# Where the weight tiles of a two-layer decoder trunk start in SBUF: offsets per weight unit, two spare tiles and one small tile removed

## The chip, the cores and the metric

The kernel runs on one core of one Trainium2 chip. The metric is the device time of one execution in microseconds (us); three runs of the kernel before gave 2567.21, 2567.60 and 2567.82 us, so the median is 2567.6 us. Five engines work side by side: TensorE (PE) multiplies matrices, ScalarE (ACT), VectorE (DVE) and GpSimd (POOL) do the elementwise work, and SyncE (SP) issues most transfers. In the profile PE has two rows: PE for the matmuls that stream a moving operand, and PEld for the loads of the stationary operand (LDWEIGHTS). Operands of both lie in SBUF, which has 128 partitions; an address below is the byte at which a tile starts in each of them. A difference of 0.2% (5.1 us) is about what a measurement of this kernel can tell from no change.

## The reference, cut to what matters

Each of two layers is a half-step feed-forward block, a mixer (attention and a state-space branch, merged by gates) and a second half-step feed-forward block. All of it is in float32; the sequence has 512 tokens, the model width is 1024, the hidden width of a feed-forward block 2816.

```python
def swiglu(h, w_up, w_down):
    gate, up = jnp.split(h @ w_up, 2, axis=-1)
    return (jax.nn.silu(gate) * up) @ w_down
...
for l in range(DEPTH):
    x = x + 0.5 * swiglu(rms_norm(x, ffn1_norm[l]), ffn1_w_up[l], ffn1_w_down[l])
    h = rms_norm(x, mix_norm[l])
    proj = h @ w_in[l]
    ...
    merged = jax.nn.sigmoid(gate_sb) * y_sb + jax.nn.sigmoid(gate_ssm) * y_ssm
    x = x + merged @ w_out[l]
    x = x + 0.5 * swiglu(rms_norm(x, ffn2_norm[l]), ffn2_w_up[l], ffn2_w_down[l])
return rms_norm(x, final_norm)
```

## The kernel before, in words

**Two halves of every operand.** Each float32 operand is held as a pair: a rounded part (`hi`, type float32r) and the rest (`lo`). A product is three matmuls into one PSUM tile (`mm3`, lines 348 to 352): L350 is `hi` times `hi`, L351 has the weights' `lo`, L352 the activations' `lo`.

**Weight units.** All weights are cut into units of at most 128 x 1024 elements, used in the order of `unit_order`. `fetch` (from L267) issues each unit's DMA into a `wraw` tile. `convert` (from L301) then writes the unit's two parts: ACT copies it to `hi` (L315, tile `whi`), DVE subtracts to get `lo` (L317, tile `wlo`). `whi` and `wlo` are tiles of the pool `wsp`, three of each, 4096 bytes per partition. `unit` hands the pair to the caller; `ahead` keeps two units converted in advance. In most stages a 128-column slice of the unit is the stationary operand and 512 columns of an activation move past it. The exceptions are the projections of v and z (`by_tokens`), where the unit moves and the activation is stationary.

**The pairs of feed-forward blocks.** 40 pairs of hidden blocks are computed with a fast matrix multiplication of seven products (`pair_of_blocks`, L604 to L677). Each product is a unit of its own, called a part: "11", "12", "s2", "s1", "s3", "s4", "22". A part has 24 matmuls of 256 moving columns (2 hidden blocks x 4 slices x 3). In parts 11, 12 and s4 the moving operand is a half of a normalised activation tile (`hhi`, `hlo`); in s2, s1, s3 and 22 it is a sum or difference of such halves (`th`, `tl`). The first part goes to PSUM tile `mm`, 12 to another `mm`, s2 and s3 to the first again, s1 and s4 to a `pa` tile, 22 to the first `mm`. For some parts the weights are themselves sums, made in tiles `s1`, `s2`, `s3` (group `s` in the profile) by POOL's accumulating DMA (L284) or DVE (L298).

**Where tiles start.** Pools are stacked from the left end of SBUF, or, where `side="right"` is given, from the right end downwards. From the left come constants, `nrm`, then `hp` (eight `hhi`, eight `hlo`), `wraw`, `wsp`, and after it whatever the stage needs: in a feed-forward block `act` and small tiles, in the mixer the gates and the pool `mp`. From the right come the eight `x` tiles, then a spare tile `rim` of 320 bytes that nothing reads or writes (L1431), then `th`, `tl`, `uv` and the sums `s`. In the mixer the right side holds instead a spare tile `edge` of 384 bytes (L1334), the attention outputs `ohi`, `olo` and 24 tiles `yt`. The built program gives these starts:

| tile | first start in bytes | remainder by 256 |
|---|---|---|
| `hhi` / `hlo` | 26208 / 42592 | 96 |
| `wraw` | 58976 | 96 |
| `whi` / `wlo` | 71264 / 83552 | 96 |
| `act` (feed-forward), first gate tile (mixer) | 95840 | 96 |
| merged `mhi` / `mlo` | 104032 / 120416 | 96 |
| sums `s` | 151200 | 160 |
| `th`, `tl` (lowest) | 171680 | 160 |
| `yt` (lowest) | 163424 | 96 |
| `ohi` / `olo` | 212576 / 220768 | 96 |
| `x` (lowest) | 212960 | 224 |

All tiles of one name lie whole multiples of 256 bytes apart, and so do the slices that a matmul takes of them (128 columns are 512 bytes), so one remainder holds for all matmuls with that tile.

**Attention.** `attention` (from L938) keeps softplus sums for four key blocks. The shortest block, 128 columns, has its two parts in one tile `short` of `mp`; matmuls L1005 and L1007 read it. Tiles `state` of `mp` (two of 768 bytes) are used later, by the state-space groups.

Of the kernel before, what the change touches and what calls it, by code (L numbers as in the profile page):

```python
# [9 lines left out]
F32R = mybir.dt.float32r  # L10
# [7 lines left out]
P = 128  # L18
SEQ = 512
NT = SEQ // P  # L20
DM = 1024
KB = DM // P
# [7 lines left out]
GW = HPG * HD  # L30
# [143 lines left out]
class Builder:  # L174
# [114 lines left out]
    def add(self, key):  # L289
# [8 lines left out]
        self.nc.vector.tensor_tensor(r, a, b, op=ALU.add)  # L298
        yield 1

    def convert(self, i):  # L301

        nc = self.nc
        key = self.keys[i]
        n = self.units[key][1] * P
        raw, self.raw[i] = self.raw[i], None
        if key[-1] in ("s1", "s3"):
            raw = self.sums[key] if key[-1] == "s1" else self.sums.pop(key)
        elif key[-1] in ("s2", "s4"):
            while key[2:] == ("pair", 0, "s4") and key not in self.sums:  # L310
                yield 1
            raw = self.sums[key[:-1] + ("s2",)]
        hi = self.t(self.wsp, [P, KB * P], "whi", F32R)
        lo = self.t(self.wsp, [P, KB * P], "wlo", F32R)
        nc.scalar.copy(hi[:, :n], raw[:, :n])  # L315
        yield 2
        nc.vector.tensor_tensor(lo[:, :n], raw[:, :n], hi[:, :n].bitcast(F32), op=ALU.subtract)  # L317
        self.loaded[i] = (hi, lo)
        if key[2:] == ("pair", 0, "s2"):
            self.spawn(self.onto(key[:-1] + ("s4",), raw), 2)  # L320
# [148 lines left out]
    def opening(self, gain):  # L469

        nc, n = self.nc, 2 * P
        raws, w = self.raw, []
        self.raw, self.loaded = [None, None], [None, None]
        for _ in raws:
            w.append((self.t(self.wsp, [P, KB * P], "whi", F32R), self.t(self.wsp, [P, KB * P], "wlo", F32R)))
        ps = [self.t(self.pa, [P, SEQ], "pa") for _ in raws]
        for k in range(KB):
            for i, (raw, (hi, lo)) in enumerate(zip(raws, w)):
                if k % 2 == 0:
                    cs = slice(k * P, k * P + n)  # L480
                    nc.scalar.copy(hi[:, cs], raw[:, cs])
                    nc.vector.tensor_tensor(lo[:, cs], raw[:, cs], hi[:, cs].bitcast(F32), op=ALU.subtract)
                if i == 0:
                    for _ in self.norm_split(k, gain):
                        pass
            ks, h = slice(k * P, k * P + P), self.h[k]
            for a, b in ((0, 0), (1, 0), (0, 1)):
                for p, parts in zip(ps, w):
                    nc.tensor.matmul(p, parts[a][:, ks], h[b], start=k + a + b == 0, stop=k == KB - 1 and b == 1)
            if k == KB - 1:  # L490
                self.ahead()
            self.tick()
            self.tick()
        self.tick()
        self.pos = 2
        return ps
# [441 lines left out]
    def attention(self, h, parts):  # L938


        nc, mp = self.nc, self.mp
# [3 lines left out]
        yield 4 if h == 0 else 2  # L945
        q, k = parts["q"], parts["k"]
        rest = self.t(mp, [P, 2, SEQ - P], "xs", F32R, bufs=3)
        short = self.t(mp, [P, 2, P], "short", F32R, bufs=1)
        spt = []
        for i in range(2):  # L950
            long = self.t(mp, [P, SEQ + 2 * P], "xs", F32R, bufs=3)
            spt.append([long[:, :SEQ], rest[:, i, :], long[:, SEQ:], short[:, i, :]])
        sums = [self.t(mp, [P, 2, SEQ - P], "y", F32R, bufs=1), self.t(self.nrm, [P, 2, SEQ - 2 * P], "acc", F32R)]
        sums = [[t[:, i, :] for i in range(2)] for t in sums]
        pzs, sps, ws, bufs, behind = {}, {}, {}, {}, {}
# [361 lines left out]
    def mixer(self, layer):  # L1317
        nc, tc = self.nc, self.tc
# [12 lines left out]
        with ExitStack() as mix:  # L1331
            enter = mix.enter_context
            branches = ExitStack()
            edge = branches.enter_context(  # L1334
                tc.tile_pool(name=f"edge{layer}", bufs=1, side="right", reuse_waits="tile"))
            self.t(edge, [P, 96], "edge")
            self.yo = branches.enter_context(
                tc.tile_pool(name=f"yo{layer}", bufs=SBH, side="right", reuse_waits="tile"))
            self.yt = branches.enter_context(
# [88 lines left out]

    def open_t(self):

        self.rim = self.tc.tile_pool(name=self.name("rim"), bufs=1, side="right", reuse_waits="tile")  # L1431
        self.t(self.rim.__enter__(), [P, 80], "rim")
        self.tpool = self.tc.tile_pool(name=self.name("tpool"), bufs=2, side="right", reuse_waits="tile")
        self.tp = self.tpool.__enter__()
        self.spool = self.tc.tile_pool(name=self.name("spool"), bufs=2, side="right", reuse_waits="tile")
        self.sx = self.spool.__enter__()

    def close_t(self):
        self.spool.__exit__(None, None, None)
        self.tpool.__exit__(None, None, None)  # L1440
        self.rim.__exit__(None, None, None)
        self.tp = None

    def build(self):
# [141 lines left out]
```

## Time and profile before

| what | us |
|---|---|
| median of three runs | 2567.6 |
| the profiled execution | 2567.14 |
| its span, first to last instruction | 2565.4 |
| PE busy | 2551.3 |
| PEld busy | 2291.4 |
| DVE busy | 1728.9 |
| ACT busy | 1281.3 |
| POOL busy | 553.7 |

The profiled execution lasted 1.74 us longer than its span, for what lies around it. Busy times of PE rows are not a sum of time that passes: a matmul's row runs until its last result is written, while the next one has begun. What passes from one matmul to the next is the difference of their starts, as the timeline view has them. The view of windows gives, for a stretch of the span, what each engine did there; instructions that reach over an end are counted in.

### The profile page before, as it was taken

To read this page: it belongs to the slowest core of one execution; us is meant where nothing else is said; L and a number is where in the kernel's file an instruction comes from. 1 tells how busy PE (TensorE), PEld (TensorE's weight loads), DVE (VectorE), ACT (ScalarE), POOL (GpSimd) and SP (SyncE) were. 2 spreads that over 40 slices of the span, in tenths; PEclk is the share of its full clock that TensorE was granted. 3 is DMA by queue.
4 is the path that set the end of the run, shared out by engine and by line. 5 is a ranking of instruction groups with operands and counts; after the bars stand their busy time and mean duration, and the time that the engine had idled before them with its cause. 6 is when DMAs were issued, how large, how long until landed. Compare 5 with 4: busy or idle time off the path is not lost.

```text
span 2565.4 us, 38502 instructions
## 1 busy us (share of the span) xinstructions
PE 2551.3 (99%) x15176; PEld 2291.4 (89%) x15176; DVE 1728.9 (67%) x2257; ACT 1281.3 (50%) x2115; POOL 553.7 (22%) x662
## 2 busy tenths in 40 slices
PE   9999999999999999999999999999999999999998
PEld 8898988888898889899998989888888888999997
DVE  8576875666564488586885858756666644876766
ACT  6343456665554265343653535566655533643434
POOL 0131301043342013131121312011533310222220
PEclk9999999999999999999999999999999999999999
DMA  6455542233333465555464545423333335656452
GB/s 188 135 150 146 133 139 82 93 120 107 102 110 102 140 196 165 164 140 158 114 180 140 157 140 139 132 80 102 117 97 104 114 111 165 188 146 168 141 163 81
DMA packets 106678, 343.14 MB, mean 134 GB/s; under 512 B 12096, under 2 KB 15616, under 8 KB 106496
## 3 DMA queue, kind: packets, MB, share of 16 engines
q1 hardware_dynamic: 93248, 294.93, 35.1%
q0 software_dynamic: 12384, 45.09, 9.9%
q8 instruction: 119, 1.95, 0.3%
q10 hardware_dynamic: 864, 0.64, 0.1%
q14 instruction: 63, 0.52, 0.1%
HBM read 327.94 MB, written 12.68 MB: 133 GB/s over the span
## 4 chain that ended last, share of the span: by engine, by line
PE 94%; DVE 3%; ACT 1%; issue 1%; DMA 0%; POOL 0%; SPq 0%; DVEq 0%; ACTq 0%; POOLq 0%
PE mm L350 26%; PE mm L352 26%; PE mm L351 26%; PE pa L350 3%; PE pa L352 3%; PE pa L351 3%; PE pa L1212 2%; PE pa L1214 1%; DVE wlo L317 1%; PE pt L890 1%; PE pt L1197 1%; PE pt L1195 1%; PE pa L890 0%; ACT whi L315 0%; PE pa L1007 0%
## 5 line engine op out<-in xcount | busy, mean ns | idle before, releaser
L315 ACT CAST whi<-wraw 128x1024 fp32r<-128x1024 f32 (+3 forms) x438 | 433.3, 989 | 655.5 <-PE mm L352 459.9
L317 DVE TENSOR_TENSOR wlo<-wraw,whi 128x1024 fp32r<-128x1024 f32 (+3 forms) x438 | 537.4, 1227 | 298.5 <-ACT whi L315 298.3
L350 PE MATMUL mm<-hhi,whi 128*128 128x512 f32 (+1 forms) x1552 | 548.8, 354 | 0.0
L352 PE MATMUL mm<-hlo,whi 128*128 128x512 f32 (+1 forms) x1552 | 537.8, 347 | 0.6 <-DVE hlo L535 0.6
L351 PE MATMUL mm<-hhi,wlo 128*128 128x512 f32 (+1 forms) x1552 | 536.7, 346 | 1.2 <-DVE wlo L317 1.2
L352 PEld LDWEIGHTS mm<-hlo,whi 128*128 128x128 f32 x1552 | 293.7, 189 | 38.1 <-DVE hlo L535 1.0
L351 PEld LDWEIGHTS mm<-hhi,wlo 128*128 128x128 f32 x1552 | 294.2, 190 | 33.9 <-DVE wlo L317 1.6
L350 PEld LDWEIGHTS mm<-hhi,whi 128*128 128x128 f32 x1552 | 294.2, 190 | 31.8
L653 POOL TENSOR_TENSOR g<-g,rs 128x512 f32<-128x512 f32 x80 | 165.1, 2066 | 552.2 <-DVE g L660 507.1
L350 PE MATMUL mm<-act,whi 128*128 128x512 f32 (+1 forms) x710 | 274.1, 386 | 0.0
L352 PE MATMUL mm<-act,whi 128*128 128x512 f32 (+1 forms) x710 | 273.8, 386 | 0.0
L351 PE MATMUL mm<-act,wlo 128*128 128x512 f32 (+1 forms) x710 | 273.6, 385 | 0.0
L350 PE MATMUL mm<-th,whi 128*128 128x256 f32 x960 | 268.9, 280 | 0.0
L351 PE MATMUL mm<-th,wlo 128*128 128x256 f32 x960 | 267.9, 279 | 0.0
L352 PE MATMUL mm<-tl,whi 128*128 128x256 f32 x960 | 267.8, 279 | 0.0
L317 DVE TENSOR_TENSOR wlo<-s,whi 128x1024 fp32r<-128x1024 f32 x160 | 234.4, 1478 | 38.3 <-ACT whi L315 35.1
L284 POOL DMA_DIRECT2D s<-in_wflat_dram x86 | 75.4, 876 | 622.2 <-DMA s<-in_wflat_dram 553.1
L681 DVE SCALAR_TENSOR_TENSOR x<-mm,x 128x512 f32<-128x512 f32 x93 | 64.1, 690 | 212.0 <-PE mm L352 212.0
L315 ACT CAST whi<-s 128x1024 fp32r<-128x1024 f32 x160 | 167.8, 1049 | 74.8 <-PE mm L352 52.8
L350 PEld LDWEIGHTS mm<-th,whi 128*128 128x128 f32 x960 | 180.5, 188 | 0.0
L352 PEld LDWEIGHTS mm<-tl,whi 128*128 128x128 f32 x960 | 180.4, 188 | 0.0
L351 PEld LDWEIGHTS mm<-th,wlo 128*128 128x128 f32 x960 | 180.0, 187 | 0.0
(305 smaller groups left out, 5119.5 us busy)
## 6 DMA issues: line engine op xcount, KB each, us to landing
wraw<-in_wflat_dram SPq DMA_DIRECT2D x326, 512.0 KB, 3.6
s<-in_wflat_dram POOLq DMA_DIRECT2D x86, 512.0 KB, 7.2
s<-in_wflat_dram SPq DMA_DIRECT2D x82, 512.0 KB, 5.0
wraw<-in_wflat_dram SPq DMA_DIRECT2D x88, 384.0 KB, 3.1
cumb<-cum_d SPq DMA_DIRECT2D x16, 768.0 KB, 4.7
xd<-x SPq DMA_DIRECT2D x16, 256.0 KB, 2.0
wraw<-in_wflat_dram SPq DMA_DIRECT2D x16, 256.0 KB, 3.1
x<-xd SPq DMA_DIRECT2D x16, 256.0 KB, 5.6
```

Of the source, the lines that this page charges most:

```text
L284: self.nc.gpsimd.dma_start(raw, self.stored(key[:-1] + (part,)), accum_op=ALU.add)
L315: nc.scalar.copy(hi[:, :n], raw[:, :n])
L317: nc.vector.tensor_tensor(lo[:, :n], raw[:, :n], hi[:, :n].bitcast(F32), op=ALU.subtract)
L350: mm(ps, a[0], b[0], start=start, stop=False, **kw)
L351: mm(ps, a[1], b[0], start=False, stop=False, **kw)
L352: mm(ps, a[0], b[1], start=False, stop=stop, **kw)
L653: eng.tensor_tensor(r, r, self.rs[:, cols].unsqueeze(1).to_broadcast([P, 2, half]), op=ALU.mult)
L681: self.nc.vector.scalar_tensor_tensor(x, pd, 0.5, x, op0=ALU.mult, op1=ALU.add)
L890: self.nc.tensor.transpose(pt[:, cs], src[:, cs], self.ident)
L1195: nc.tensor.matmul(pc[:, :P], bt[:, span(c)], ct[:, span(c)], start=True, stop=True)
L1197: nc.tensor.matmul(pu, btok[:, c, :], xws[c].rearrange("p h d -> p (h d)"), start=True, stop=True)
L1212: nc.tensor.matmul(py[:, i * HD:(i + 1) * HD], decs[c][:, i, :], xdts[c][:, i, :], start=True, stop=True)
```

## The change

A new method `parts_of` gives `convert` and the kernel's opening their `whi` and `wlo` tiles. The tiles are 64 elements (256 bytes) longer, and the unit is written, and later read, from an offset `at` inside them, in elements of four bytes: 48 (192 bytes) for the parts 11, 12 and s4 of a pair, 16 (64 bytes) for the other four parts, 32 (128 bytes) for the units of the two branch projections, 0 for all else. The spare tiles `edge` and `rim` are dropped, and `short` is replaced by two tiles of the tag `state`. No instruction is added or removed, and none changes its place in any queue.

```diff
+    def parts_of(self, key):
+
+        if "pair" in key:
+            at = 48 if key[-1] in ("11", "12", "s4") else 16
+        else:
+            at = 32 if key[1] in ("bsb", "bssm") else 0
+        return [self.t(self.wsp, [P, KB * P + 64], tag, F32R)[:, at:] for tag in ("whi", "wlo")]
...
-        hi = self.t(self.wsp, [P, KB * P], "whi", F32R)
-        lo = self.t(self.wsp, [P, KB * P], "wlo", F32R)
+        hi, lo = self.parts_of(key)
...
-            w.append((self.t(self.wsp, [P, KB * P], "whi", F32R), self.t(self.wsp, [P, KB * P], "wlo", F32R)))
+            w.append(self.parts_of(self.keys[0]))
...
-        short = self.t(mp, [P, 2, P], "short", F32R, bufs=1)
+        short = [self.t(mp, [P, GW], "state", F32R)[:, :P] for _ in range(2)]
...
-            spt.append([long[:, :SEQ], rest[:, i, :], long[:, SEQ:], short[:, i, :]])
+            spt.append([long[:, :SEQ], rest[:, i, :], long[:, SEQ:], short[i]])
...
-            edge = branches.enter_context(
-                tc.tile_pool(name=f"edge{layer}", bufs=1, side="right", reuse_waits="tile"))
-            self.t(edge, [P, 96], "edge")
...
-        self.rim = self.tc.tile_pool(name=self.name("rim"), bufs=1, side="right", reuse_waits="tile")
-        self.t(self.rim.__enter__(), [P, 80], "rim")
...
-        self.rim.__exit__(None, None, None)
```

## The prediction

> **What bounds the kernel now.** I read the page's busy times first, then the chain that ended last.
>
> ```profile
> span 2565.4 us, 38502 instructions
> PE 2551.3 (99%) x15176; PEld 2291.4 (89%) x15176; DVE 1728.9 (67%) x2257; ACT 1281.3 (50%) x2115; POOL 553.7 (22%) x662
> PE 94%; DVE 3%; ACT 1%; issue 1%; DMA 0%; POOL 0%; SPq 0%; DVEq 0%; ACTq 0%; POOLq 0%
> ```
>
> PE is busy from end to end, and 94% of the chain is its own. The view of waits, for PE alone, says whether anything keeps it waiting:
>
> ```profile
> PE mm L351 <- DVE wlo L317: 1.2, 1, 1.2
> PE pt L1464 <- DVE ones L505: 1.1, 1, 1.1
> PE pa L1007 <- DVE short L444: 0.8, 2, 0.4
> PE mm L352 <- DVE hlo L535: 0.6, 1, 0.6
> PE pa L350 <- ACT c L669: 0.3, 1, 0.3
> PE pt L728 <- ACT g L716: 0.2, 1, 0.2
> ```
>
> These are all of its waits, 4.2 us. So time can go only where matmuls follow one another faster or slower, and what counts is the distance between their starts. Next I look at one pair of feed-forward blocks, early and late in the span, with windows cut at the first matmul of each kind of moving operand (parts 11 and 12 together; s2, s1, s3; s4):
>
> ```profile
> 299.91:305.67 5.76, 5.76 (x50) 1.00 0.26 73
> 305.67:314.16 8.49, 8.49 (x75) 1.00 0.17 46
> 314.16:317.04 2.88, 2.88 (x27) 1.00 0.49 139
> 2499.66:2505.42 5.76, 5.76 (x50) 1.00 0.23 68
> 2505.42:2513.91 8.49, 8.49 (x75) 1.00 0.16 48
> 2513.91:2516.79 2.88, 2.88 (x27) 1.00 0.44 137
> ```
>
> The columns are the window, its PE time with the count of matmuls touched (two or three neighbours included), granted clock, DMA share and GB/s. The code has 48, 72 and 24 matmuls there. So the parts that move `hhi`/`hlo` take 5.76/48 = 2.88/24 = 0.1200 us per matmul, and the parts that move `th`/`tl` 8.49/72 = 0.1179. Shape, clock (1.00) and weights path are the same, the two pairs 2200 us apart agree to the last digit, and both kinds write `mm` and `pa`. **The two kinds differ by 2.1 ns per matmul**, and by where the moving operand starts against the stationary one: by the table of starts, moving minus stationary, modulo 256, is 96-96 = 0 for `hhi`/`hlo` and 160-96 = 64 for `th`/`tl`.
>
> The timeline shows how a part begins and that a load runs beside the matmul before it:
>
> ```profile
> 299.91 0.29 PE L350 MATMUL mm<-hhi,whi 128*128 128x256 f32 x1
> 299.91 0.19 PEld L351 LDWEIGHTS mm<-hhi,wlo 128*128 128x128 f32 x1
> 300.04 0.28 PE L351 MATMUL mm<-hhi,wlo 128*128 128x256 f32 x1
> 300.15 0.29 PE L352 MATMUL mm<-hlo,whi 128*128 128x256 f32 x1
> 300.28 0.28 PE L350 MATMUL mm<-hhi,whi 128*128 128x256 f32 x1
> 300.39 0.28 PE L351 MATMUL mm<-hhi,wlo 128*128 128x256 f32 x1
> 300.51 0.28 PE L352 MATMUL mm<-hlo,whi 128*128 128x256 f32 x1
> ...
> 305.67 0.28 PE L350 MATMUL mm<-th,whi 128*128 128x256 f32 x1
> 305.79 0.28 PE L351 MATMUL mm<-th,wlo 128*128 128x256 f32 x1
> ```
>
> The load of the next weights starts with the current matmul (both at 299.91). The first steps into a run of `hhi` are 130, 110, 130, 110 ns before it settles at 120. Two streams that fall into step with each other look like that; an operand that is slow by itself would be slow by the same amount from its first matmul.
>
> **The change part by part.**
>
> *Distances after.* `wsp` grows by 6 x 256 bytes, so all to its right on the left side moves by 1536 = 6 x 256 and keeps its remainder. Without `rim` (320 bytes) `th` and `tl` start 320 higher, remainder 160+320-256 = 224; without `edge` (384) `yt`, `ohi`, `olo` go to 96+384-256 = 224. Parts 11, 12, s4 have weights at 96+192-256 = 32: moving minus stationary becomes 96-32 = **64**. Parts s2, s1, s3, 22 have them at 96+64 = 160: 224-160 = **64**, as before. The branch units: 224-(96+128) = 0, as before. All others: 96-96 = 0, as before. So the one relation that changes for many matmuls is that of parts 11, 12 and s4, from 0 to the distance at which the same shape takes 117.9 ns.
>
> *How many.* By the groups, forms kept apart:
>
> ```profile
> L350 PE MATMUL mm<-th,whi 128*128 128x256 f32 x960 | 268.9, 280 | 0.0
> L350 PE MATMUL mm<-hhi,whi 128*128 128x256 f32 x640 | 181.1, 283 | 0.0
> L350 PE MATMUL pa<-hhi,whi 128*128 128x256 f32 x320 | 90.8, 284 | 0.4 <-ACT c L669 0.3
> ```
>
> 640+320 = 960 of L350, and as many of L351 and L352: 2880 matmuls, 40 pairs of 72. Per pair they take 5.76+2.88 = 8.64 us, at the other pace 72 x 0.1179 = 8.49: 0.15 us less, and **40 x 0.15 = 6.0 us**. The rows' own durations differ by more, 283 against 280 ns; with 3 ns it would be 8.6 us, but a row reaches into the next matmul, so what passes is the difference of starts, and I take that.
>
> *Borders between parts.* At four of the seven borders of a pair (12 to s2, s3 to s4, s4 to 22, 22 to what follows) a load of the new offset runs beside a matmul of the old operand, at 96-160 or 224-32, both 192 modulo 256: no row shows that distance. From below: nothing. From above: that each begins like the run at 299.91, whose first five steps take 0.60 us against 5 x 0.1179 = 0.59, about 0.011 us; 160 borders make 1.8 us. I take nothing, since only one load in 24 is concerned, and since the entry into `hhi` that costs this today goes away; both ends stay in the range.
>
> *Tiles 4352 instead of 4096 bytes apart.* Distances by 512 or more now differ among the three buffers. The first z unit shows this: its slices start 448 elements, 1792 = 7 x 256 bytes, apart, so they lie at 0 and 256 modulo 512 from the stationary operand in turns.
>
> ```profile
> 438.57 0.35 PE L350 MATMUL mm<-whi,hhi 128*128 128x408 f32 x1
> 439.13 0.34 PE L350 MATMUL mm<-whi,hhi 128*128 128x408 f32 x1
> 439.68 0.35 PE L350 MATMUL mm<-whi,hhi 128*128 128x408 f32 x1
> ```
>
> Three matmuls of the one take 0.56 us, of the other 0.55: nothing.
>
> *Conversions.* They write and read at other offsets.
>
> ```profile
> L317 DVE TENSOR_TENSOR wlo<-wraw,whi 128x1024 fp32r<-128x1024 f32 x326 | 428.3, 1314 | 192.5 <-ACT whi L315 192.5
> L315 ACT CAST whi<-wraw 128x1024 fp32r<-128x1024 f32 x326 | 342.2, 1050 | 471.9 <-PE mm L352 315.0 <-PE pa L352 66.2 <-issue 64.0
> L315 ACT CAST whi<-s 128x1024 fp32r<-128x1024 f32 x160 | 167.8, 1049 | 74.8 <-PE mm L352 52.8 <-ACT whi L315 16.1 <-issue 5.5
> 299.79 0.28 PE L352 MATMUL mm<-tl,whi 128*128 128x256 f32 x1
> 299.92 1.22 DVE L317 TENSOR_TENSOR wlo<-wraw,whi 128x1024 fp32r<-128x1024 f32 x1
> 299.91:319.87 19.96, 19.96 (x170) 19.96 (x169) 17.81 (x19) 10.48 (x14) 5.48 (x3) 1.00 0.28 81
> ```
>
> ACT's copy takes 1050 ns from `wraw` (0 apart from `whi`) and 1049 from `s` (64 apart): no effect of placement. In the last row the fourth number is DVE's busy time in a whole pair, 17.81 of 19.96 us: 2.15 us free. It has seven subtractions there, so each of 1.22 us would have to take 0.31 us (25%) more before DVE becomes the bound. I cost this at nothing; that slack covers it, and the pair's 0.15 us less leaves 2.0 us of it.
>
> *`short` as two `state` tiles.* Same number of instructions; each half waits for readers of its own. Today's wait there is 0.8 us (the row L1007 above), so it can give or cost about that; I take nothing. The attention's products of weights with v get 128 apart instead of 0: 96 of them (4 heads x 4 key blocks x 3 matmuls x 2 layers), at 2.1 ns 0.2 us either way. `edge` and `rim` have no instruction. Nothing is moved past any queue.
>
> **Sum.** 2567.14 - 6.0 = 2561.1 for the profiled execution. The median shown is 0.46 above it, so the forecast is 2567.6 - 6.0 = **2561.6 us**.
>
> **The rivals.**
>
> *No change: the difference is not in the distance.* It could lie in the tiles themselves (`th` lies far to the right, `hhi` near the left). Then every matmul keeps its pace: 2567.6 us. For it speaks that the trace has only these two cases. The Trainium skill, "TensorE: Matmul & The Clock Gate", section "Step-by-step: what each phase is for", states that the stream and the weight load have independent read ports, so that loading the next weights does not take read bandwidth from the running matmul; by that the change would give 0. Against this rival, and not in agreement with that rule, stand the 2.1 ns and the settling at 299.91.
>
> *Slower: the moving operand's own start decides.* If remainder 160 is what makes `th` and `tl` quick, not the distance, then they lose it: they move to 224, and `hhi` stays at 96. If 224 acts like 96 (both are 96 modulo 128), four parts of each pair fall to the slower pace: 40 x 96 x 2.1 ns = 8.1 us, 2575.7 us. It decides from the first part s2: its 24 matmuls would take 2.88 us instead of 2.83. Today's trace cannot exclude it, since all stationary operands there have the same remainder; the settling over several steps speaks against it.
>
> *Borders.* The distance works, but each of the 160 borders costs its upper end: 2561.6 + 1.8 = 2563.4 us, a gain of 0.16%.
>
> **How the numbers follow.** Forecast 0.67, borders 0.10, no change 0.13, moving start 0.08, something not listed, new waits on DVE above all, 0.02. The forecast's own range is 2560.5 to 2562.8 (rounding of 0.01 us in the two windows of a pair is 0.4 us over 40, the waits of attention 0.8). With borders it holds 0.77, too little, so the range reaches to no change and the scatter of its runs: 2560.0 to 2567.9. Faster by over 0.2% (5.1 us, about what a measurement of this kernel can tell) is nearly all of the forecast, 0.64, and a part of borders, 0.02: 0.66. Same is the rest of the forecast and of borders and no change, 0.24. Slower is the moving start and the unlisted: 0.10.
>
> **What would show it.** Right: parts 11 and 12 in about 5.66 us instead of 5.76, s4 in 2.83 instead of 2.88, and s2, s1, s3 still in 8.49; PE's waits still a few us in all. Wrong: `hhi` parts at 5.76 (no change), `th` parts at 8.64 (moving start), first steps of s2 or 22 over 120 ns (borders), or new waits on `wlo` with DVE at 19.8 us a pair.

## The result and the profile after

The changed kernel takes 2561.8 us (median of 11 runs, 2560.42 to 2563.3), the kernel before 2567.6 us (11 runs beside them, 2567.19 to 2568.57). The ratio is 0.9976 with a 95% interval of 0.9968 to 0.9984, so 4.1 to 8.2 us less; forecast were 2561.6 us and 6.0 us less. The profiled execution of the changed kernel is one of 2561.8 us.

The page after begins like the one before, only shorter:

```profile
span 2560.1 us, 38503 instructions
PE 2545.7 (99%) x15176; PEld 2285.2 (89%) x15176; DVE 1728.6 (68%) x2257; ACT 1280.9 (50%) x2115; POOL 557.8 (22%) x662
```

The one instruction more is a semaphore instruction of SyncE (551 of them, before 550); the counts of the five rows are the same. DVE and ACT do the same work in the same time; the 5.3 us of span go with 5.6 us less PE busy time. The windows of the same two pairs of blocks, cut as before (parts 11 and 12; s2, s1, s3; s4):

```profile
299.84:305.49 5.65, 5.65 (x50) 1.00 0.25 70
305.49:313.97 8.48, 8.48 (x74) 1.00 0.14 46
313.97:316.80 2.83, 2.83 (x27) 1.00 0.51 143
2494.50:2500.16 5.66, 5.66 (x51) 1.00 0.22 69
2500.16:2508.63 8.47, 8.47 (x74) 1.00 0.17 48
2508.63:2511.46 2.83, 2.83 (x26) 1.00 0.46 139
```

Parts 11 and 12 went from 5.76 to 5.65 us and s4 from 2.88 to 2.83: 5.65/48 = 2.83/24 = 117.8 ns per matmul, the pace that `th` and `tl` had and keep (8.48/72). The timeline, which prints starts to 10 ns, shows that the uneven entry is gone too: after the first matmul of part 11 the steps are 120, 110, 120, 120, 120 ns where they were 130, 110, 130, 110, 120.

```profile
299.84 0.28 PE L357 MATMUL mm<-hhi,whi 128*128 128x256 f32 x1
299.96 0.28 PE L358 MATMUL mm<-hhi,wlo 128*128 128x256 f32 x1
300.07 0.28 PE L359 MATMUL mm<-hlo,whi 128*128 128x256 f32 x1
300.19 0.28 PE L357 MATMUL mm<-hhi,whi 128*128 128x256 f32 x1
300.31 0.28 PE L358 MATMUL mm<-hhi,wlo 128*128 128x256 f32 x1
300.43 0.28 PE L359 MATMUL mm<-hlo,whi 128*128 128x256 f32 x1
```

The whole pair, with part 22, goes from 19.96 to 19.78 us, and DVE's busy time in it stays at 17.81:

```profile
299.84:319.62 19.78, 19.78 (x170) 19.78 (x169) 17.81 (x19) 10.47 (x14) 5.66 (x3) 1.00 0.26 80
```

PE's waits are as few as before. The largest and the one that the new `state` tiles could have changed:

```profile
PE mm L358 <- DVE wlo L324: 1.6, 1, 1.6
PE pa L1014 <- DVE state L451: 0.8, 2, 0.4
```

The two mixers, where the distances are as they were but for the attention's products of weights with v, take the same time to 0.2 us. First the kernel before, then the changed one:

```profile
352.55:897.39 544.84, 544.38 (x2744) 1.00 0.33 107
1623.67:2168.55 544.88, 544.42 (x2744) 1.00 0.35 106
```

```profile
352.28:897.27 544.99, 544.54 (x2745) 1.00 0.33 107
1619.95:2164.90 544.95, 544.50 (x2744) 1.00 0.34 106
```

One thing hides part of the gain in this execution: its opening. The first matmul of the first pair starts at 74.27 us, before it was 73.11:

```profile
73.11 0.28 PE L350 MATMUL mm<-hhi,whi 128*128 128x256 f32 x1
```

```profile
74.27 0.28 PE L357 MATMUL mm<-hhi,whi 128*128 128x256 f32 x1
```

In the seven runs below that have the same opening code this start lies between 72.84 and 73.59 us, so it scatters by about a microsecond. From there on the changed kernel gained 5.3 + 1.16 = 6.5 us.

### The profile page after: what moved, and what is told of

Its sections match the earlier page's. It is cut to its first block, busy times and chain, and to the rows that moved or that the text cites. A ratio compares the mean times of both kernels' runs of the same rounds, so it can differ in the third digit from the quotient of the medians.

```text
span 2560.1 us, 38503 instructions
## 1 busy us (share of the span) xinstructions
PE 2545.7 (99%) x15176; PEld 2285.2 (89%) x15176; DVE 1728.6 (68%) x2257; ACT 1280.9 (50%) x2115; POOL 557.8 (22%) x662
## 4 chain that ended last, share of the span: by engine, by line
PE 94%; DVE 3%; ACT 1%; issue 1%; DMA 1%; POOL 0%; SPq 0%; DVEq 0%; ACTq 0%; POOLq 0%
PE mm L357 26%; PE mm L359 26%; PE mm L358 26%; PE pa L357 3%; PE pa L358 3%; PE pa L359 3%; PE pa L1219 2%; DVE wlo L324 1%; PE pa L1221 1%; PE pt L897 1%; PE pt L1204 1%; PE pt L1202 1%; ACT whi L322 0%; PE pa L897 0%; PE pa L1014 0%
```

## The experiments

The theory: PE's pace in a stream of 256-column matmuls depends on the distance, modulo 256 bytes, between the start of the moving operand and that of the stationary one; at 0 a step takes 120 ns, at 64 it takes 117.8. The rivals were the rest of the change (layout, pads), the moving tile or its own start, and which of several distances is good. All kernels differ from the changed one in `parts_of` alone. Offsets there are in elements of four bytes; "h parts" are 11, 12 and s4 (moving `hhi`, `hlo`), "t parts" the other four (moving `th`, `tl`). With `hhi` at remainder 96 and `th` at 224, an offset `at` gives h parts the distance 0 - 4 at and t parts 128 - 4 at, modulo 256. From the run with all parts at 192 on, the edits have further lines that name the other kinds of unit; where nothing is said of these, they leave them as in the changed kernel. Each kernel has one trace. "The 36 pairs" are those in which s2, s1 and s3 follow each other without other matmuls between them; their paces are taken from all starts of that trace.

**The gain undone, the rest kept.**

```diff
-            at = 48 if key[-1] in ("11", "12", "s4") else 16
+            at = 0 if key[-1] in ("11", "12", "s4") else 16
```

> Weights of parts 11, 12 and s4 written at offset 0 of their tiles (everything else as in the changed kernel), so that moving minus stationary start is 0 again for them and stays 64 for the other four parts. If the distance makes the gain: parts 11 and 12 of a pair take 5.76 us again, s4 2.88, s2 to s3 still 8.49, and the time is that of the kernel before, 2567 to 2568.5 us. If the gain came from the rest of the change (dropped spare tiles, longer weight tiles, another layout): about 2561.8 us, with these parts at 5.66 and 2.83.

Measured: 2567.14 us (11 runs), ratio to the kernel before 0.9997 (0.9989 to 1.0006). Windows, cut as above:

```profile
300.06:305.81 5.75, 5.75 (x50) 1.00 0.22 68
305.81:314.29 8.48, 8.48 (x74) 1.00 0.15 46
314.29:317.16 2.87, 2.87 (x26) 1.00 0.50 141
```

The h parts are back at about 120 ns, and the gain is gone to within the 0.5 us that the medians differ. Longer tiles, dropped pads and the `state` tiles bring nothing that this shows.

**The loss moved to the other operand.**

```diff
-            at = 48 if key[-1] in ("11", "12", "s4") else 16
+            at = 48 if key[-1] in ("11", "12", "s4") else 32
```

> Weights of parts s2, s1, s3 and 22 written 128 bytes into their tiles, so that their start has the same remainder as that of the moving th and tl (distance 0); parts 11, 12 and s4 stay at distance 64. By the distance: s2 to s3 of a pair take 8.64 us or a little more instead of 8.49, with uneven first steps, and the time is 2561.8 + 3840 x 2.1 ns = about 2570 us. If what makes these parts quick is the tile th or its own start: they keep 8.49 and the time stays at 2561.8 us.

Measured: 2568.74 us (11 runs), ratio 1.0004 (0.9995 to 1.0013), 6.9 us above the changed kernel.

```profile
299.82:305.48 5.66, 5.66 (x50) 1.00 0.24 69
305.48:314.11 8.63, 8.63 (x75) 1.00 0.13 46
314.11:316.94 2.83, 2.83 (x27) 1.00 0.49 143
```

Now `th` and `tl`, at the very same place as in the changed kernel, take 8.63/72 = 119.9 ns, and `hhi`, at the place it always had, 117.9. So neither the moving tile nor its own start decides. Nor does the start of the weights by itself: in the kernel before, both kinds had it at remainder 96 and their paces differed. What is left is the relation of the two. The time came out about 1 us below the estimate; behind the opening (72.84 us here, 74.27 in the changed kernel) this profile is 2493.5 - 2485.8 = 7.7 us longer than the changed kernel's, against 3840 x 2.1 ns = 8.1 us expected.

**Distances 128 and 192.**

```diff
-            at = 48 if key[-1] in ("11", "12", "s4") else 16
+            at = 32 if key[-1] in ("11", "12", "s4") else 48
```

> Distances no run has shown: 128 for parts 11, 12 and s4 (weights 128 bytes into their tiles), 192 for s2, s1, s3 and 22 (192 bytes into theirs). If only distance 0 is slow: every part at 117.9 ns per matmul and about 2562 us. If the cost falls off with the distance in both directions: 192 as 64, 128 the quickest, below 117.9 ns for 11, 12 and s4 (5.66 us or less for the first two). If what counts is that the load runs ahead of or behind the matmul: 192 is slow like 0, 8.64 us for s2 to s3, about 2570 us.

Measured: 2561.12 us (one run). Parts 11 and 12, then s2, s1, s3 of the pair near 300 us:

```profile
299.21:304.90 5.69, 5.69 (x51) 1.00 0.21 69
304.90:313.38 8.48, 8.48 (x75) 1.00 0.15 46
```

Parts 11 and 12 (distance 128) take 118.5 ns per matmul here, and over the 36 pairs 118.5 to 120.2, 119.0 in the mean, so between 64 and 0. s2, s1, s3 (192) take 8.48 us here, but 8.17 in 9 of the 36 pairs. None of the three expectations fits in full: the cost is no simple function of the distance.

**Other distances for 512 columns.**

```diff
+        elif "down" in key:
+            at = 48
+        elif key[1] in ("bsb", "bssm"):
+            at = 48
+        elif key[1] == "out":
+            at = 16
         else:
-            at = 32 if key[1] in ("bsb", "bssm") else 0
+            at = 0 if key[1] in ("v", "z") else 32
```

> The units with 512 moving columns, all at distance 0 in both kernels, get other distances: 64 for the down projections, 192 for the two branch projections and the output projection, 128 for q, k, x, b, c, the gates and the plain gate and up units. v and z stay at 0, the pairs at 64. If a 512-column matmul gains like a 256-column one (2.1 ns): some 9000 of them, about 19 us less, 2543 us. If its longer stream hides the load anyway: 2561.8 us and 226.7 ns from start to start as before. Slower by some us would mean that distance 0 is the good one for the long stream.

Measured: 2582.89 us (5 runs), ratio 1.0059 (1.0047 to 1.0072). Windows of 24 matmuls each, at distance 128 (plain gate and up units), 64 (down), 192 (branch), 192 (output), and the same 24 in the kernel before, all at 0:

```profile
34.46:40.06 5.60, 5.60 (x26) 1.00 0.08 31
341.18:346.67 5.49, 5.49 (x25) 1.00 0.57 184
823.22:828.82 5.60, 5.60 (x26) 1.00 0.29 87
2221.06:2226.66 5.60, 5.60 (x26) 1.00 0.84 275
```

```profile
34.35:39.79 5.44, 5.44 (x26) 1.00 0.14 56
340.31:345.75 5.44, 5.44 (x26) 1.00 0.62 209
817.83:823.27 5.44, 5.44 (x25) 1.00 0.25 72
2205.27:2210.71 5.44, 5.44 (x25) 1.00 0.78 283
```

This is the third expectation: for 512 columns distance 0 is the best of these, with 226.7 ns per matmul, 228.8 at 64, 233.3 at 128 and 192. The distance counts there as well, with the opposite sign.

**All parts at 192.**

```diff
-            at = 48 if key[-1] in ("11", "12", "s4") else 16
+            at = 16 if key[-1] in ("11", "12", "s4") else 48
```

> The two offsets of the pairs exchanged (64 bytes for parts 11, 12 and s4, 192 for the other four), so that all seven parts are at distance 192, which the run with distances 128 and 192 showed to be a little quicker for s2, s1, s3 and 22 than 64 (about 3 us less over all of them). If 192 does the same for parts 11, 12 and s4, at 1 ns per matmul: 3 us + 2880 x 1 ns = 6 us less than the changed kernel, about 2556 us. If that gain came from the mixture of two distances or from the borders: nearer to 2561 us.

Measured: 2550.07 us (5 runs, 2549.81 to 2551.29), ratio to the kernel before 0.9932 (0.9918 to 0.9945): **better than both kernels**, and 6 us better than expected. In 34 of the 36 pairs the h parts are not quicker than at 64 (5.66 us); the t parts are, but not always. s2, s1, s3 of two pairs that follow each other:

```profile
263.34:271.81 8.47, 8.47 (x74) 1.00 0.65 154
283.05:291.23 8.18, 8.18 (x75) 1.00 0.50 100
```

There are two paces at one distance, 8.47/72 = 117.6 and 8.18/72 = 113.6 ns, and nothing between; in these three parts 24 of the 36 pairs have the quick one. All 10 pairs that come first after other units have the slow one; of the 26 that follow another pair, all but two, which lie near 2250 us, have the quick one.

Part 22, also at 192, is quick (about 114.3 ns) in 34 of the 36 pairs, those that come first among them. And in the two pairs near 2250 us it is the other way round: there the h parts are quick and the t parts are slow. Parts 11 and 12; s2, s1, s3; s4; 22 of the first of them:

```profile
2239.87:2245.33 5.46, 5.46 (x50) 1.00 0.54 192
2245.33:2253.82 8.49, 8.49 (x75) 1.00 0.46 105
2253.82:2256.56 2.74, 2.74 (x26) 1.00 1.05 173
2256.56:2259.39 2.83, 2.83 (x26) 1.00 0.87 266
```

So at 192 either operand can have the quick pace (5.46/48 = 113.8 ns for `hhi`); in none of the 36 pairs do both have it.

**Only `wlo` at distance 0.**

```diff
-            at = 48 if key[-1] in ("11", "12", "s4") else 16
+            at, lo = (48, 0) if key[-1] in ("11", "12", "s4") else (16, 32)
...
-        return [self.t(self.wsp, [P, KB * P + 64], tag, F32R)[:, at:] for tag in ("whi", "wlo")]
+        return [self.t(self.wsp, [P, KB * P + 64], tag, F32R)[:, a:] for tag, a in (("whi", at), ("wlo", lo))]
```

> In the pairs, whi stays at distance 64 and wlo goes to distance 0. Each group of three matmuls then has one that uses wlo (L358 in the changed kernel's numbering) and one beside which wlo is loaded (the one before it, L357). If the load of the next weights meets the running matmul, the step that begins at L357 is long (about 120 ns) and the other two short; if a matmul's own weights count, it is the step that begins at L358. In all about a third of the loss: 6700 x 2.1 / 3 = 4.7 us, 2566.5 us. If a cost arises only where the two streams stay in step over several matmuls: no loss, 2561.8 us.

Measured: 2562.31 us (one run).

```profile
299.12:304.77 5.65, 5.65 (x50) 1.00 0.24 73
304.77:313.25 8.48, 8.48 (x75) 1.00 0.16 46
```

A third of the steps at distance 0 costs nothing that shows (5.65 and 8.48 us, as in the changed kernel): the third expectation. So the cost is not one of a single matmul; it comes when all of them are at distance 0. The run can't say, then, whether the load of the next weights or the matmul's own stationary operand is the partner; that stays open.

**Two sweeps.** Of their edits the lines for the pairs, first and second sweep (the other kinds of unit got the distances that the expectations name):

```diff
+            at = 8 if key[-1] in ("11", "12", "s4") else 56
...
+            at = 56 if key[-1] in ("11", "12", "s4") else 40
```

> One look at distances no run has shown, each on its own kind of unit: parts 11, 12, s4 at 224; s2, s1, s3, 22 at 160; down projections at 32; q, k, x, b, c, gates and plain gate and up at 224; branches at 16; output projection at 240. If the cost for 256 columns falls steadily from 0 over 64 to 192: 160 between 64 and 192 (117.5 ns), 224 the quickest (under 116.5). If 512 columns lose with growing distance (64: about 2 ns, 128: 4, 192: 6.5): the small ones, 16 and 32, cost under 1 ns, 224 and 240 over 6, or, if the distance counts in both directions, under 1 as well.

> The same with other distances: parts 11, 12, s4 at 32; s2, s1, s3, 22 at 224; down projections at 240; q, k, x, b, c, gates and plain gate and up at 16; branches at 224; output projection at 32. With the first sweep each of 16, 32, 224 and 240 stands on two kinds of unit: if the distance is what counts and not the tile, the two agree within 0.5 ns per matmul (224 on the pairs: 11, 12, s4 there, the other four here).

Measured: 2594.58 and 2582.98 us (one run each); the loss is again in the 512-column units. For 256 columns, parts 11 and 12 and then s2, s1, s3; first sweep (224 and 160), second sweep (32 and 224):

```profile
304.22:309.90 5.68, 5.68 (x50) 1.00 0.22 69
309.90:318.44 8.54, 8.54 (x74) 1.00 0.15 46
```

```profile
302.23:307.84 5.61, 5.61 (x50) 1.00 0.37 100
307.84:316.35 8.51, 8.51 (x74) 1.00 0.17 46
```

Distance 224 gives 5.68/48 = 118.3 ns with one tile and 8.51/72 = 118.2 with the other: the distance counts, not the tile. The first sweep's expectation for 256 columns missed: 224 is not the quickest (under 116.5 was expected), and 160 does not lie between 64 and 192. Per matmul: 0: 120.0, 32: 116.9, 64: 117.8, 128: 118.5 to 120.2, 160: 118.6, 192: 117.6 or 113.6, 224: 118.3.

For 512 columns, 24 matmuls each: first sweep, branches (16) and down (32); second sweep, plain gate and up (16) and output (32):

```profile
897.19:902.67 5.48, 5.48 (x26) 1.00 0.29 96
100.97:106.57 5.60, 5.60 (x26) 1.00 0.14 56
```

```profile
35.84:41.32 5.48, 5.48 (x25) 1.00 0.02 6
908.75:914.35 5.60, 5.60 (x25) 1.00 0.98 275
```

At 16 it is 228.3 ns with both tiles, at 32 it is 233.3 (under 1 ns of loss was expected of these two), and 224 and 240 take 5.60 us, 233.3 ns, as well, each on two kinds of unit. So the distance counts here too, and not the tile; the loss does not grow steadily with it, since 64 (5.49 us) costs less than 32.

**What precedes the t parts at 192.** Two runs with the t parts at 192 and the h parts at 64 and at 32:

```diff
-            at = 48 if key[-1] in ("11", "12", "s4") else 16
+            at = 48 if key[-1] in ("11", "12", "s4") else 48
```

> All parts of a pair written 192 bytes into their tiles: 11, 12 and s4 at distance 64 as in the changed kernel, the other four at 192. It asks where the gain of the run with all parts at 192 (11.7 us below the changed kernel, nearly all of it in th and tl at about 114 ns in most of its parts) comes from. If 192 on th and tl alone makes it: about 10 to 11 us below the changed kernel, 2551 us. If th and tl fall into the quick pace only when they follow parts at 192: they stay near 117, 3 us below the changed kernel, 2558.5 us, as with 128 before them.

```diff
-            at = 48 if key[-1] in ("11", "12", "s4") else 16
+            at = 56 if key[-1] in ("11", "12", "s4") else 48
```

> Parts 11, 12 and s4 at distance 32 (116.8 ns per matmul in the second sweep, 117.5 at 192), the other four at 192. If the pace of th and tl depends on their own distance only: 2550.1 - 2880 x 0.7 ns = 2548 us. If it depends on the parts before them, as the run with distances 64 and 192 asks too: between 2548 and 2557 us, with th and tl at 116 to 117 ns.

Measured: 2560.03 us (7 runs, ratio 0.9970, 0.9958 to 0.9981) and 2554.76 us (5 runs, 0.9948, 0.9936 to 0.9961). In both only 4 of the 36 pairs have s2, s1, s3 in the quick pace. Part 22 is quick in 4 pairs of the first run but in 32 of the second, as in this one (s2, s1, s3, then 22):

```profile
303.59:312.08 8.49, 8.49 (x75) 1.00 0.14 46
314.88:317.62 2.74, 2.74 (x26) 1.00 0.51 139
```

So the own distance does not settle it. With the h parts at 192, 128, 64 and 32 the quick pace comes in 24, 9, 4 and 4 pairs for s2, s1, s3, and in 34, 0, 4 and 32 for part 22. Only the offset of the h parts differs between these runs, so these parts have a say in the pace of the t parts that follow them. What exactly chooses was not found.

## Why the prediction was right

- **The step that carried it**, reading 2.1 ns between two kinds of the same matmul as an effect of the distance between starts, held: undoing the distance alone lost the gain again (2567.14 us), and moving distance 0 to the other operand moved the loss there.
- **The size** was right: parts 11, 12 and s4 lost 0.11 + 0.05 us a pair against the 0.15 forecast, and the profiled execution gained 6.5 us behind its opening against 6.0. The medians differ by 5.8 us, 0.2 below the forecast. That it came so close is in part luck: openings alone scatter by about a microsecond. The interval, 4.1 to 8.2 us, leaves open whether the gain is over the 5.1 us that the prediction took as its mark for faster. (The lower end of the forecast's own range follows from its two terms as 2561.6 - 0.4 - 0.8 = 2560.4, not 2560.5; nothing hangs on it.)
- **Starts, not durations.** The rows' durations would have given 8.6 us; the difference of starts was the right measure.
- **Costed at nothing, and nothing came:** the borders between parts (the whole pair lost 0.18 us, no less than the 0.16 of its three windows), tiles 4352 bytes apart (the mixers stay at 545 us), the conversions (DVE 1728.9 and 1728.6 us in all), `state` for `short` (0.8 us of wait in both).
- **The rivals.** The tile itself and the moving operand's own start both fell with the run that put the t parts at 0. The rule of the Trainium skill, "TensorE: Matmul & The Clock Gate", section "Step-by-step: what each phase is for", by which the load of the next weights does not take read bandwidth from the running matmul, spoke for the rival "no change". That rival is refuted: the placement of the weights alone is worth 2567.14 - 2561.8 = 5.3 us here. Whether it is the load's reads that meet the stream's, and so whether the rule itself fails, no run here shows.
- **Streams that fall into step**, argued from the first steps of a run of `hhi`, is supported by the two paces at 192, by the run with `wlo` alone at 0, and by the steps in single nanoseconds: at distance 0 they are 128, 117, 125, 113 and then 120 each to the end of parts 11 and 12 (kernel before, from 299.91 us), and for s2, s1, s3 put at 0 they are 118, 119, 121, 117, 117 and then 120 each, while in parts 11 and 12 at 64 (changed kernel) they go on changing between 117 and 119. It was not shown directly: no view has the reads themselves.

## What to carry to other kernels

Where PE is busy without a wait and equal matmuls differ by a few nanoseconds from start to start, compare where their operands begin, modulo 256 bytes, and sort the starts by that. (The 256 was not tested by itself. The three buffers of the changed kernel, 17 x 256 bytes apart, give one pace, 117.7 to 117.8 ns in parts 11 and 12 of the 36 pairs; with 128 in its place, the distances 0 and 128 would have to act alike, and for 512 columns they differ by 6.6 ns.) An offset in the weight tile cost 256 bytes a tile and no instruction of PE; but the best distance must be tried for each moving length, since 64 instead of 0 gains 2 ns for 256 columns and costs 2 ns for 512. Once one distance has helped, try the others too: exchanging the two offsets here gained another 11.7 us.

## What the hardware showed beyond expectation

- The same distance can have two stable paces (113.6 and 117.6 ns at 192), and which one a run gets depends on the distance of the matmuls before it (s2, s1, s3 are quick in 24, 9, 4 and 4 of 36 pairs with these at 192, 128, 64 and 32).
- For 512 columns the sign is reversed: 5.44 us for 24 matmuls at distance 0, 5.48 at 16, 5.49 at 64, 5.60 at 32, 128, 192, 224 and 240.
- A cost that a whole run of matmuls at distance 0 pays (2.1 ns each) vanishes when only every third weight tile is at 0.
